# A hybrid encoder layer on one core: the second piece's token combinations made from DRAM during the first piece, the kept weights one per block, and the projection's block sums split over VectorE and GpSimd

## The chip, the cores and the metric

The kernel runs on one core of a Trainium2 chip. The metric is the device time of one execution in microseconds (us), a median over several executions. Engines are named as in the profile: PE is TensorE, PEld its weight loads, DVE or V is VectorE, ACT or S is ScalarE, POOL or G is GpSimd, SP or Q is SyncE, which only issues transfers. In the source, `V`, `S`, `G` and `Q` are the handles of these four engines, so `S.dma_start` issues a transfer from ScalarE's queue and `G.dma_start` one from GpSimd's.

## The reference, cut to what matters

One layer over 2048 prompt tokens and 32 sample tokens, in f32: a projection, attention and a gated linear attention (GLA) side by side, an output projection and a feed-forward network (FFN).

```python
z = rmsnorm(x, g_mix) @ w_in                     # D_MODEL = 1024
h = x + concat(attention(z), gla(z)) @ w_out     # 1024 x 1024
y = h + relu(rmsnorm(h, g_ffn) @ w_up)**2 @ w_down   # D_FF = 4096
```

## The kernel before, in words

Every f32 product is made as three products of rounded parts (high x high, high x low, low x high), so each operand exists as a pair of tiles whose names end in `h` and `l`. The high part is a copy by ACT, the low part a subtraction on V or POOL (`weights`, `load_tok`, `load_mix`).

The 2080 tokens are cut into three pieces p of two groups each: piece 0 has groups of 328 tokens, pieces 1 and 2 groups of 356. The FFN takes the pieces in the order `ORDER = (1, 2, 0)`, so the piece with index 2 is its second. Projection and FFN have these parts:

- **Output projection** (`op_phase`). Six groups j = 0 to 5, for (p, gi) in order; group 0's product is made earlier. For each of eight row blocks f: 24 matmuls, then V adds the residual input y (loaded by `load_y` from SP, one group ahead), ACT squares, V sums the squares into `acc`. y has three buffers, of which one is shared with memory of the stage before. `next_mix` converts the next group's attention output into `mx0` or `mx1`. After a group, `post` makes 1/rms (`oprb`, `rsqrt`), scales y (L1210) and stores what the FFN reads. It is a generator, and its parts run between the next group's steps; for the last group they run inside the FFN.
- **Token combinations.** The FFN multiplies 2 x 2 block matrices with seven products in place of eight. On the token side these are B11, B21, B22 and four differences T1 to T4. For gi = 0 `post` stores the scaled halves B11 and B21. For gi = 1 it makes all differences on V (L1220) with two copies by ACT per step, and stores T3, T1, B22, T2, T4 to the DRAM tensors `Td`.
- **Weight sums of w_down.** The weight side needs sums S1 to S4 of each of the 16 blocks b. `block_sums` makes them with four subtractions or additions on POOL and they are stored to `sd`: four early blocks and five (`MIDDLE`) in the stages before the projection (`down_sums`), the remaining seven, 9 to 15, in the projection, one begun every four steps f, all loads, sums and stores on POOL.
- **FFN** (`ffn_phase`). For each piece 16 blocks. A block has seven steps of `up` (U) and seven of `down` (D), in turn, each with 12 matmuls. After each step `prepare` makes one more pair of weights, six steps ahead: loads on SP, high part on ACT, low part on POOL, but for two of the seven down weights (`wf_dXA`, the steps 0 and 5) of the first piece's blocks 0 to 13, whose low part is made by V at L1390. The down results are added by V to the accumulators P in SBUF (L1520; L1615 copies in block 0), whose memory is shared with the tiles of the projection.
- **Kept weights.** The pairs of the last block, 15, are made once and kept in DRAM. `keep_last` makes them in four parts, in blocks 9 to 12 of the first piece, with one, two, two and two weights; the sources go through the ring `xa` of two buffers, which also carries the sources of the current down weights.
- **Start of the FFN.** In the first four down steps only one of the two PSUM buffers (`ps2[1]`) is used, since the remaining parts of `post` still use the other's banks.

The order on each engine is that of a planner that places the instructions as the code gives them with estimated times; tiles that share memory add waits.

## Time and profile before

| | us |
|---|---|
| median of three runs | 2279.6 (2277.75, 2279.6, 2291.31) |
| the profiled execution | 2273.34 |
| its span in the trace | 2271.6 |
| projection, about | 712 to 918 |
| FFN, first piece | 918 to 1425 |
| FFN, second and third piece | 1425 to 2272 |

All times of rows are microseconds from the start of the span. A row of a timeline gives the start, the busy time, the engine, the line and the tiles, how many instructions it joins, and in brackets how long the engine had been idle before it and which instruction or transfer ended that. A row of the windows gives the busy time of each engine with its instruction count, the granted clock of PE and the share and rate of the transfers.

### The profile page before, as it was taken

Reading aid. Unit: us, or ns where it says so; the run is one execution under the profiler, and the core shown is the slowest. Engines: PE = TensorE matmul, PEld = TensorE weight load, DVE = VectorE, ACT = ScalarE, POOL = GpSimd, SP = SyncE. Lnnn points to the kernel's source line nnn. Section 1 sums busy time; section 2 is a strip of 40 time slices with the busy share of each in tenths; the row PEclk is TensorE's granted clock in tenths of the full one; section 3 lists DMA queues with packets and bytes.
Section 4 is the critical chain, followed back from the end, with each engine's and each line's share of the span. In section 5 each row is a group of like instructions: output and inputs, shape, how many; then the busy total and the mean of one; then the engine's idle time right before and its main releaser. Section 6 shows DMA issues by size and latency. Waiting matters only on the chain.

```text
span 2271.6 us, 40566 instructions
## 1 busy us (share of the span) xinstructions
PE 2156.1 (95%) x14790; PEld 2023.4 (89%) x14790; DVE 1586.8 (70%) x3440; ACT 1232.3 (54%) x2728; POOL 1537.3 (68%) x1430
## 2 busy tenths in 40 slices
PE   7999999989989889799999999999999989999996
PEld 5777777778878889699999899999999989999996
DVE  8776666878887436667777776566666666766676
ACT  3545555655662212556666566665555656666662
POOL 7662224662443743678888789888887898888884
PEclk9999999989999999899999999999999999999998
DMA  7642454452235877534445547444444574444433
GB/s 257 222 173 92 153 182 153 180 179 81 101 100 193 299 252 270 215 117 140 134 138 158 172 146 294 146 142 134 140 144 132 164 267 144 140 155 146 148 112 113
DMA packets 195546, 376.34 MB, mean 166 GB/s; under 512 B 43265, under 2 KB 120370, under 8 KB 189970
## 3 DMA queue, kind: packets, MB, share of 16 engines
q1 hardware_dynamic: 172754, 293.02, 40.0%
q0 software_dynamic: 12608, 50.90, 5.9%
q10 hardware_dynamic: 9984, 29.82, 3.4%
q8 instruction: 117, 1.92, 0.4%
q14 instruction: 83, 0.68, 0.1%
HBM read 278.70 MB, written 94.98 MB: 165 GB/s over the span
## 4 chain that ended last, share of the span: by engine, by line
PE 80%; DVE 7%; DMA 5%; POOL 3%; issue 3%; ACT 2%; SPq 1%; DVEq 0%; ACTq 0%; POOLq 0%
PE dn L157 26%; PE u L157 26%; PE op L157 7%; PE zq L157 5%; PE zv L157 3%; PE zr L157 3%; PE zkv L157 2%; PE zk L157 2%; PE go L157 1%; PE O L157 1%; PE A L157 1%; DVE P L1520 1%; PE S L157 1%; SPq L60 1%; PE pT L161 1%
## 5 line engine op out<-in xcount | busy, mean ns | idle before, releaser
L1520 DVE TENSOR_TENSOR P<-P,dn 128x712 f32<-128x712 f32 (+1 forms) x642 | 559.2, 875 | 235.8 <-PE dn L157 220.2
L44 ACT ACTIVATE u<-u 128x356 f32<-128x356 f32 (+1 forms) x384 | 174.1, 453 | 58.0 <-DVE u L1520 33.9
L44 ACT ACTIVATE r<-u 128x356 f32<-128x356 f32 (+1 forms) x192 | 88.6, 462 | 137.3 <-PE u L157 137.3
L1520 DVE TENSOR_TENSOR u<-u,r 128x356 f32<-128x356 f32 (+1 forms) x144 | 75.6, 525 | 118.3 <-PE u L157 118.2
L944 POOL TENSOR_TENSOR E<-cc 128x256 f32<-128x256 f32 (+1 forms) x117 | 68.8, 624 | 92.9 <-DVE cc L796 59.7
L1415 POOL TENSOR_TENSOR stage<-stage 128x512 f32<-128x512 f32 x92 | 119.8, 1302 | 13.4 <-DMA stage<-in_w_up 8.5
L713 POOL TENSOR_TENSOR sd<-sd 128x128 f32<-128x128 f32 (+2 forms) x132 | 101.1, 782 | 29.2 <-DMA sd<-in_w_down 26.6
L1020 DVE COPY_PREDICATED AT<-masks,A 64x64 f32<-64x64 int32 (+1 forms) x330 | 82.7, 252 | 26.2 <-ACT AT L44 17.0
L1621 POOL TENSOR_TENSOR P<-P,P 128x712 f32<-128x712 f32 (+1 forms) x38 | 64.9, 1729 | 22.7 <-DVE P L1520 22.5
L44 ACT ACTIVATE P<-S,negm 128x192 f32<-128x192 f32 (+2 forms) x128 | 51.6, 417 | 46.4 <-DVE negm L578 40.9
L1283 DVE TENSOR_TENSOR y<-op,y 128x356 f32<-128x356 f32 (+1 forms) x48 | 25.0, 536 | 65.7 <-PE op L157 39.0
L44 ACT ACTIVATE E<-E 128x1024 f32<-128x1024 f32 (+2 forms) x68 | 67.3, 1013 | 1.1
L596 POOL TENSOR_TENSOR P<-P,es 128x512 f32<-128x512 f32 x15 | 15.8, 1050 | 64.2 <-ACT sq L44 22.7
L44 ACT ACTIVATE op<-y 128x356 f32<-128x356 f32 (+1 forms) x42 | 19.4, 468 | 62.2 <-DVE y L1283 62.1
L955 DVE TENSOR_TENSOR E<-E,kq 128x256 f32<-128x256 f32 (+1 forms) x117 | 52.7, 503 | 0.5 <-ACT E L44 0.3
L44 ACT ACTIVATE pS<-pT 128x256 f32<-128x256 f32 (+1 forms) x62 | 27.2, 490 | 43.7 <-PE pT L161 43.2
L1520 DVE TENSOR_TENSOR u<-u,f 128x356 f32<-128x356 f32 (+1 forms) x96 | 49.8, 519 | 0.6 <-ACT u L44 0.4
L720 POOL DMA_DIRECT2D sd<-in_w_down x56 | 36.3, 652 | 15.6 <-DMA sd<-sd 10.5
L44 ACT ACTIVATE v<-go 128x256 f32<-128x256 f32 (+1 forms) x34 | 12.8, 380 | 60.3 <-DVE Sp L1052 26.2
L577 DVE TENSOR_REDUCE mx<-S 128x2 f32<-128x384 f32 (+2 forms) x64 | 32.8, 535 | 16.9 <-PE S L157 16.6
L44 ACT ACTIVATE f<-u 128x356 f32<-128x356 f32 (+1 forms) x96 | 43.7, 455 | 0.0
L1647 POOL TENSOR_TENSOR P<-P,stage 128x712 f32<-128x712 f32 (+1 forms) x24 | 41.5, 1729 | 1.5 <-DVE P L1520 1.5
(1921 smaller groups left out, 8917.6 us busy)
## 6 DMA issues: line engine op xcount, KB each, us to landing
stage<-in_w_up SPq DMA_DIRECT2D x92, 512.0 KB, 4.0
stage<-sd SPq DMA_DIRECT2D x92, 512.0 KB, 4.6
stage<-in_w_down SPq DMA_DIRECT2D x46, 512.0 KB, 3.6
stage<-su SPq DMA_DIRECT2D x30, 512.0 KB, 3.7
sd<-in_w_down POOLq DMA_DIRECT2D x24, 512.0 KB, 6.9
sd<-sd POOLq DMA_DIRECT2D x12, 1024.0 KB, 6.5
stage<-in_w_down SPq DMA_DIRECT2D x46, 256.0 KB, 3.0
xT1a<-in_xT_prompt SPq DMA_DIRECT2D x16, 512.0 KB, 5.1
```

What stands on the lines that cost most here:

```text
L44: ins = f(*args, **kw)
L157: self._pe(self.T.matmul(out, lhsT, rhs, start=start, stop=stop, **kw), ns)
L577: V.reduce_max(mx[:, ch, us], sp, axis=AX.X)
L713: self.G.tensor_tensor(out=o, in0=x, in1=y, op=op)
L720: self.G.dma_start(raw[:, k], w[b, :, k, :, c0 : c0 + n])
L944: G.tensor_tensor(out=e4, in0=c4, in1=ref, op=ALU.subtract)
L955: V.tensor_tensor(out=e4, in0=e4, in1=halves_of(kq, L, m), op=ALU.mult)
L1020: V.copy_predicated(dst, mk.unsqueeze(1).broadcast_to([L // nh, 2, w // m, m]), src[r].rearrange("s p (n m) -> s p n m", m=m),)
L1415: tt = lambda o, x, y, op: G.tensor_tensor(out=o, in0=x, in1=y, op=op)
L1520: add = lambda out, x, y, op=ALU.add: V.tensor_tensor(out=out, in0=x, in1=y, op=op)
L1621: eng.tensor_tensor(out=e.acc[q][:, j : j + 2], in0=e.acc[q][:, j : j + 2], in1=e.acc[x][:, j : j + 2], op=ALU.add)
L1647: G.tensor_tensor(out=at, in0=at, in1=waiting.pop(g), op=ALU.add)
```

## The change

Five edits. (1) `EARLY` block sums in the GLA stage are spawned one step later with other spacing; all engines' instructions stand in the same order up to the place where the sixth block appears. (2) `MIDDLE` is 6: block 9's sums move from the projection into the GLA stage. The six blocks left in the projection are begun at other steps, four of them on VectorE and two on GpSimd, and all their loads and stores are issued by ScalarE. (3) `load_y(0, 0)` is issued after the last load of the stage before. (4) For the FFN's second piece (index 2, `LATE`), `post` only scales and stores B22 and B12, the two halves of the second group. T1 to T4 are made in blocks 10 to 13 of the first piece by `combine`: for one row block k each, four loads, four subtractions on GpSimd and four stores. With it, the start of the FFN uses both PSUM buffers. (5) `keep_last` makes one weight per block in blocks 3 to 9, through the general ring of input tiles.

```diff
-ORDER = (1, 2, 0)
-EARLY, MIDDLE = 4, 5
+ORDER, LATE = (1, 2, 0), 2
+EARLY, MIDDLE = 4, 6
...
-                if i == 3:
+                if i == 4:
...
-                        self.spawn(self.down_sums(early[j::2], one, 1, 2500), 14000 * j)
+                        self.spawn(self.down_sums(early[j::2], one, 1, 3500), 13000 * j)
...
-                self.G.tensor_tensor(out=o, in0=x, in1=y, op=op)
+                (eng or self.G).tensor_tensor(out=o, in0=x, in1=y, op=op)
...
+            if p == LATE:
+                for f in (*range(H, KB), *range(H)):
+                    scaled(y[:, f], f)
+                yield
+                S.dma_start(Td["B22"], y[:, H:])
+                S.dma_start(Td["B12"], y[:, :H])
+                return
...
-        for n, b in enumerate(range(EARLY + MIDDLE, self.NB)):
-            at = KB + 4 * n
-            steps.setdefault(at, []).append(lambda b=b: begin(b))
+        when = ((8, V), (12, V), (18, G), (24, V), (28, V), (33, G))
+        for (at, eng), b in zip(when, range(EARLY + MIDDLE, self.NB), strict=True):
+            steps.setdefault(at, []).append(lambda b=b, eng=eng: begin(b, eng))
...
-            steps.setdefault(at + 6, []).append(lambda b=b: end(b))
+            steps.setdefault(at + 5, []).append(lambda b=b: end(b))
...
-            self.load_block(x, b, 0, 512)
-            sums[b] = x, self.block_sums(x)
+            self.load_block(x, b, 0, 512, S)
+            sums[b] = x, self.block_sums(x, 1, eng)
...
-            G.dma_start(self.sd[b], sums.pop(b)[0].rearrange("p k m n -> p (k m) n"))
-
-        load_y(0, 0)
+            S.dma_start(self.sd[b], sums.pop(b)[0].rearrange("p k m n -> p (k m) n"))
+
+        with tc.issue_after(self.last_load):
+            load_y(0, 0)
...
-            pending = post(p, gi, acc, stage(f"T3{p}", N) if gi else None)
+            pending = post(p, gi, acc, stage(f"T3{p}", N) if gi and p != LATE else None)
...
+            def keep_last(i):
+
+                b, x = NF - 1, DOWN[i][0]
+                m = "S2 S3 S4 S1".split().index(x) if x[0] == "S" else int(x[1]) - 1
+                src = self.sd[b][:, m : m + 1] if x[0] == "S" else w_dn[b, :, int(x[2]) - 1 : int(x[2]), 512 * m : 512 * m + 512]
+                weights(f"d{b}{x}", load(src), True, G)
...
-                    two = ps2[1] if g == 0 and i < 4 else ps2[j // 2]
-                    ps = two.tile([P, 2, 512], F32, tag="two", name=f"dn{g}_{q}_{j}")
+                    ps = ps2[j // 2].tile([P, 2, 512], F32, tag="two", name=f"dn{g}_{q}_{j}")
...
+            def combine(k, i):
+
+                N, T = self.size(pieces[LATE][0]), self.Td[LATE]
+                names = (("B12", "B22"), ("B11", "B21"))
+                if i == 1:
+                    for pair in names:
+                        x = self.io_tile("quads")[:, : 2 * N].rearrange("p (m t) -> p m t", m=2)
+                        for j, q in enumerate(pair):
+                            quads[q] = x[:, j]
+                            Q.dma_start(x[:, j], T[q][:, k])
+                if i == 3:
+                    b12, b22, b11, b21 = (quads[q] for pair in names for q in pair)
+                    for o, x, y in ((b11, b12, b11), (b12, b22, b12), (b22, b22, b11), (b21, b21, b22)):
+                        G.tensor_tensor(out=o, in0=x, in1=y, op=ALU.subtract)
+                if i == 6:
+                    for q, t in (("B11", "T1"), ("B12", "T3"), ("B22", "T2"), ("B21", "T4")):
+                        Q.dma_start(T[t][:, k], quads.pop(q))
...
-                    if g == 0 and i in (0, 2):
+                    if g == 0 and i in (0, 2, 5):
                         next(self.pending, None)
...
-                    if g == 0 and i < 4:
-                        next(self.pending, None)
-                    if n == 0 and 9 <= b < 13 and i == 3:
-                        keep_last(b - 9)
+                    if n == 0 and 3 <= b < 10 and i == 3:
+                        keep_last(b - 3)
+                    if n == 0 and 10 <= b < 10 + H:
+                        combine(b - 10, i)
```

Three places show how the instructions move. In the rows, the name before the arrow is written and those behind it are read; the number after a name tells its copies apart.

SP's queue in the GLA stage before: y is the residual input of the projection's group 0, caf and g are inputs of the GLA tiles that follow, and y has the first place behind the normed tokens nTb.

```order
L60 DMA nTb_4l<-nTl_92 128x2048
L60 DMA y_9175<-in_xT_prompt 128x8x128
L60 DMA caf_6456<-ca_109 96x128
L60 DMA g_6081<-rgd_126 128x512
L60 DMA caf_6456<-ca_110 96x128
L60 DMA y_9175<-in_xT_prompt 128x8x128
L60 DMA y_9175<-in_xT_prompt 128x8x40
L60 DMA y_9175<-in_xT_sample 128x8x32
L60 DMA g_6615<-rgd_127 128x512
```

The same place in the changed kernel:

```order
L60 DMA nTb_4l<-nTl_92 128x2048
L60 DMA caf_6457<-ca_109 96x128
L60 DMA caf_6457<-ca_110 96x128
L60 DMA g_6082<-rgd_126 128x512
L60 DMA g_6616<-rgd_127 128x512
```

The four transfers of y(0, 0) now stand some 35 rows later, behind the last load of w_out and the GLA state's last store.

VectorE at the projection's first steps with matmuls (group 1) in the changed kernel: `op` is a product in PSUM, y_9202 the group's residual input, `sd` the block sums (L713), and `oprb` with `rsq` the 1/rms of group 0. In the kernel before, the same rows stand there without those of `sd` (such sums were on GpSimd).

```order
L1285 TENSOR_TENSOR acc_9193<-acc_9193,op_6_9105 128x328 x2
L713 TENSOR_TENSOR sd_9256<-sd_9256 128x512
L1282 TENSOR_TENSOR y_9202<-op_1_0_9224,y_9202 128x328
L713 TENSOR_TENSOR sd_9256<-sd_9256 128x512 x3
L713 TENSOR_TENSOR sd_9424<-sd_9424 128x512
L1282 TENSOR_TENSOR y_9202<-op_1_1_9259,y_9202 128x328
L713 TENSOR_TENSOR sd_9424<-sd_9424 128x512
L1203 TENSOR_SCALAR oprb<-oprb 82x4
L1285 TENSOR_TENSOR acc_9223<-acc_9223,op_1_1_9259 128x328
L713 TENSOR_TENSOR sd_9424<-sd_9424 128x512
L243 TENSOR_SCALAR oprb<-oprb 82x4
L713 TENSOR_TENSOR sd_9424<-sd_9424 128x512
```

The eight sums of two blocks now stand between the adds of y and the first steps of 1/rms on this engine.

VectorE at the start of the FFN before: the scaling (L1210) and the differences (L1220) of the last group alternate with the FFN's own work, low parts of tokens (T3l, B22l, T4l) and of squared activations (uB11l).

```order
L1518 TENSOR_TENSOR T3l<-T3l,T3h 128x712
L1210 SCALAR_TENSOR_TENSOR opa<-y_10282,packed,oprb 128x356
L1220 TENSOR_TENSOR y_10282<-opa,y_9858 128x356
L1520 TENSOR_TENSOR uB11l<-u_1_10936,uB11h 128x356
L1210 SCALAR_TENSOR_TENSOR y_10282<-y_10282,packed,oprb 128x356
L1518 TENSOR_TENSOR B22l<-B22l,B22h 128x712
L1220 TENSOR_TENSOR opa<-y_10282,opa 128x356
L1520 TENSOR_TENSOR u_2_11047<-u_0_10900,r_10735 128x356
L1518 TENSOR_TENSOR T4l<-T4l,T4h 128x712
```

The same place in the changed kernel:

```order
L1511 TENSOR_TENSOR B22l<-B22l,B22h 128x712
L1210 SCALAR_TENSOR_TENSOR y_10288<-y_10288,packed,oprb 128x356 x8
L1513 TENSOR_TENSOR uB11l<-u_1_10940,uB11h 128x356
L1513 TENSOR_TENSOR u_2_11027<-u_0_10904,r_10739 128x356
L1511 TENSOR_TENSOR T4l<-T4l,T4h 128x712
L1513 TENSOR_TENSOR u_3_10998<-u_3_10998,r_10738 128x356
```

The 16 rows of L1220 are gone, and the eight scalings stand in one piece ahead of uB11l, u_2 and T4l.

More of the change, by code (lines that the diff above doesn't have):

```diff
@@ L91, in __init__ @@
         self.Td = [
-            {x: dt([P, KB // 2, n], f"Td{p}{x}") for x in ("B11", "B21", "T2", "T1", "T3", "B22", "T4")}
+            {x: dt([P, KB // 2, n], f"Td{p}{x}") for x in ("B11", "B21", "T2", "T1", "T3", "B22", "T4", "B12")[: 8 if p == LATE else 7]}
             for p, n in enumerate(sizes)
@@ L704, in load_gla_consts, with block_sums @@
         self.gla_consts = masks, d0, wal, bal, one, ones
-    def block_sums(self, raw, parts=1):
+    def block_sums(self, raw, parts=1, eng=None):
         n = raw.shape[-1] // parts
@@ L712, in block_sums, with load_block @@
             for o, x, y, op in ((a22, a21, a22, ALU.add), (a21, a11, a21, ALU.subtract), (a11, a22, a11, ALU.subtract), (a12, a12, a11, ALU.subtract)):
-                self.G.tensor_tensor(out=o, in0=x, in1=y, op=op)
+                (eng or self.G).tensor_tensor(out=o, in0=x, in1=y, op=op)
                 yield
-    def load_block(self, raw, b, c0, n):
+    def load_block(self, raw, b, c0, n, queue=None):
         w = self.a["w_down"].rearrange("(b k p) (m n) -> b p k m n", k=2, p=P, m=2)
         for k in range(2):
-            self.G.dma_start(raw[:, k], w[b, :, k, :, c0 : c0 + n])
+            (queue or self.G).dma_start(raw[:, k], w[b, :, k, :, c0 : c0 + n])
     def down_sums(self, units, tile_, parts, step):
@@ L1229, in post, with begin @@
                 tt(y0[:, H + k], y0[:, H + k], A)
-            last = p == 2
             yield
-            eng = Q if last else S
-            eng.dma_start(Td["T3"], t3)
-            if last:
-                yield
-            eng.dma_start(Td["T1"], y[:, :H])
-            eng.dma_start(Td["B22"], y[:, H:])
-            if last:
-                yield
-            eng.dma_start(Td["T2"], y0[:, :H])
-            eng.dma_start(Td["T4"], y0[:, H:])
+            for x, src in (("T3", t3), ("T1", y[:, :H]), ("B22", y[:, H:]), ("T2", y0[:, :H]), ("T4", y0[:, H:])):
+                S.dma_start(Td[x], src)
         mix = {(0, gi): self.mix[gi] for gi in range(2)}
         steps = {}
-        for n, b in enumerate(range(EARLY + MIDDLE, self.NB)):
-            at = KB + 4 * n
-            steps.setdefault(at, []).append(lambda b=b: begin(b))
+        when = ((8, V), (12, V), (18, G), (24, V), (28, V), (33, G))
+        for (at, eng), b in zip(when, range(EARLY + MIDDLE, self.NB), strict=True):
+            steps.setdefault(at, []).append(lambda b=b, eng=eng: begin(b, eng))
             for i in (2, 3):
                 steps.setdefault(at + i, []).append(lambda b=b: more(b))
-            steps.setdefault(at + 6, []).append(lambda b=b: end(b))
+            steps.setdefault(at + 5, []).append(lambda b=b: end(b))
         sums = {}
-        def begin(b):
+        def begin(b, eng):
             x = xp.tile([P, 2048 + PADX], F32, tag="x", name=f"sd{b}")[:, :2048].rearrange("p (k m n) -> p k m n", k=2, m=2)
-            self.load_block(x, b, 0, 512)
-            sums[b] = x, self.block_sums(x)
+            self.load_block(x, b, 0, 512, S)
+            sums[b] = x, self.block_sums(x, 1, eng)
         def more(b):
@@ L1458, in up_weights @@
                 yield
-            def keep_last(part):
-                b = NF - 1
-                if part == 0:
-                    s = load(w_dn[b, :, 0:1, :512], True)
-                    weights(f"d{b}A11", s, True, G)
-                    return
-                s = load(w_dn[b, :, 1:2, :] if part == 3 else self.sd[b][:, 2 * (part == 1) : 2 * (part == 1) + 2], True)
-                names = (("S4", "S1"), ("S2", "S3"), ("A12", "A22"))[part - 1]
-                cut = (s[:, :, :512], s[:, :, 512:]) if part == 3 else (s[:, 0:1], s[:, 1:2])
-                for x, src in zip(names, cut):
-                    weights(f"d{b}{x}", src, True, G)
+            def keep_last(i):
[3 more added lines that the diff above has]
+                weights(f"d{b}{x}", load(src), True, G)
             def down_weights(n, b, out):
@@ L1633, in ffn_phase @@
             rest = [(q, gi, f) for q, gi, f0 in ((3, 1, 0), (5, 1, H), (2, 0, 0), (4, 0, H)) for f in (f0, f0 + 2)]
-            waiting = {}
+            waiting, quads = {}, {}
+            def combine(k, i):
[14 more added lines that the diff above has]
+                        Q.dma_start(T[t][:, k], quads.pop(q))
             def residual(g, i):
```

## The prediction

> **What bounds the kernel now.** I read the page first, its busy times and the chain that ended last.
>
> ```profile
> PE 2156.1 (95%) x14790; PEld 2023.4 (89%) x14790; DVE 1586.8 (70%) x3440; ACT 1232.3 (54%) x2728; POOL 1537.3 (68%) x1430
> PE 80%; DVE 7%; DMA 5%; POOL 3%; issue 3%; ACT 2%; SPq 1%; DVEq 0%; ACTq 0%; POOLq 0%
> ```
>
> TensorE (PE) is busy 95% of the span, and 80% of the chain that ended last is its matmuls. The change alters no matmul, so it can win only what PE idles and what the restarts behind idle times cost. The windows show where that is:
>
> ```profile
> 495.00:520.00 25.00, 18.20 (x182) 15.28 (x177) 15.93 (x57) 10.21 (x20) 11.71 (x18) 0.80 0.37 97
> 712.00:780.00 68.00, 58.81 (x370) 57.60 (x370) 28.45 (x70) 15.55 (x29) 48.41 (x46) 0.92 0.94 310
> 780.00:832.00 52.00, 46.17 (x293) 45.87 (x291) 23.02 (x56) 9.04 (x18) 25.40 (x23) 0.97 0.93 322
> 920.00:960.00 40.00, 31.53 (x154) 29.88 (x154) 26.06 (x58) 25.67 (x54) 30.10 (x25) 0.83 0.55 197
> 960.00:1020.00 60.00, 53.82 (x318) 53.52 (x319) 34.39 (x52) 33.08 (x68) 38.67 (x32) 0.94 0.41 144
> 1020.00:1100.00 80.00, 80.00 (x495) 80.00 (x494) 59.74 (x90) 48.29 (x102) 66.65 (x54) 1.00 0.45 143
> 1240.00:1330.00 90.00, 83.12 (x484) 82.23 (x483) 67.94 (x85) 50.04 (x107) 69.13 (x60) 0.94 0.51 167
> 1330.00:1420.00 90.00, 87.84 (x539) 87.28 (x539) 63.90 (x94) 54.91 (x113) 88.43 (x63) 1.00 0.65 234
> ```
>
> The columns are the stretch, its length, the busy time and count of PE, its loads, DVE, ACT and POOL, the granted clock, and the transfers' share and GB/s. In a quiet stretch (1020 to 1100) PE is full and there is nothing to win. The stretches the change touches leave 6.8 us idle in GLA (495 to 520), 9.2 and 5.8 in the projection, 8.5 and 6.2 at the start of the feed-forward network, and 6.9 at 1240 to 1330. The price of a restart comes from the row of the chain behind a long gap:
>
> ```profile
> 834.47 15.57 PE op L157 x80
> ```
>
> At the rate of the quiet stretch (495 matmuls in 80.00 us, 0.162 each) 80 would take 12.9 us; behind the gap they took 15.57. A restart costs up to about 2.6 us beside the gap. Twelve matmuls, a step of the network, are 1.94 us, and a block's 14 steps 27.
>
> **Early sums and y(0, 0).** The early block sums only change steps, and no engine's order changes by it up to the GLA stage: 0. In the GLA stage, y(0, 0) leaves the head of SP's queue:
>
> ```profile
> 490.44 0.56 POOL L730 DMA_DIRECT2D sd<-sd  x1 [0.30 <-POOL sd L713]
> 485.16 0.38 SPq L60 DMA_DIRECT2D nTb_4l<-nTl  x1
> 496.10 0.62 SPq L60 DMA_DIRECT2D y<-in_xT_prompt  x1
> 496.82 0.93 SPq L60 DMA_DIRECT2D caf<-ca  x1
> 497.91 3.65 DMA g<-rgd
> 501.58 0.63 ACT L44 ACTIVATE g<-g 128x512 f32<-128x512 f32 x1 [5.79 <-DMA g<-rgd]
> 503.96 0.79 PE L157 MATMUL go<-Sp,Qc 64*128 64x128 f32 x2 [6.80 <-ACT kdT L44]
> ```
>
> SP issues nothing from 485.54 to 496.10, because y's memory is that of the block sums whose store left at 490.44. Everything behind it is late: g lands at 501.56, ACT was idle 5.79 us for it, kdT stands behind g on ACT, and PE, waiting for kdT, idles 6.80. With y gone, caf and g can go some 10 us earlier, more than the gap, which should vanish. I take −8, the gap and half a restart; the ends are −9.4 (gap and full restart) and −4 (part of ACT's idle time replaced by another wait). Block 9's sums come into this stage on POOL: eight additions of 0.8 us (the next fence) in a stage where POOL has slack; I put 0, at most +2.
>
> **Block sums of the projection.** Rows of POOL's share of it and of the same operation on V:
>
> ```profile
> 483.75 6.40 POOL L713 TENSOR_TENSOR sd<-sd 128x256 f32<-128x256 f32 x8 [4.19 <-DMA sd<-in_w_down]
> 732.48 8.91 POOL L713 TENSOR_TENSOR sd<-sd 128x512 f32<-128x512 f32 x7
> 727.37 4.59 DVE L1286 TENSOR_TENSOR acc<-acc,op 128x328 f32<-128x328 f32 x3
> L1390 DVE TENSOR_TENSOR wf_d11A<-stage,wf_d11A x2: 685/3404/6123, 1251.1 to 1268.0; 128x512 fp32r<-128x512 f32 x2
> ```
>
> POOL gives up 28 additions of 1.28 us and keeps 8 of them. V gets 16; its own price for two inputs of 128x512 in SBUF is 0.69 us undisturbed, 11 us in all, in stretches where it is busy 28.45 of 68 and 23.02 of 52 us, so throughput hides them. But in group 1 eight of them stand ahead of 1/rms of group 0, for which PE waits, and their loads are now issued by ACT behind other transfers. Beside POOL's sums three such instructions of V took 1.53 us each, so the eight can also take 12. Between 0 and +5.5 (8 x 0.69) in group 1 I take +2. The twelve loads and six stores cost ACT's queue an issue each (0.4 to 0.9 us in SP's rows above), beside an ACT busy 15.55 of 68 us: 0.
>
> mx0 is written by ACT and POOL when the memory is free after group 1; POOL no longer has its DMA issues in between: −1, between −3 and +3 (ACT now issues them).
>
> The big gap of the projection follows from SP's queue and the full transfer engines:
>
> ```profile
> 805.34 8.62 SPq L60 DMA_DIRECT2D y<-in_xT_prompt  x4
> 814.06 1.73 SPq L60 DMA_DIRECT2D m<-mixT  x1
> 815.88 1.99 SPq L60 DMA_DIRECT2D stage<-in_w_up  x2
> 817.97 11.00 SPq L60 DMA_DIRECT2D y<-in_xT_prompt  x4
> 833.89 2.70 DVE L1283 TENSOR_TENSOR y<-op,y 128x356 f32<-128x356 f32 x6 [15.40 <-DMA y<-in_xT_prompt]
> 834.47 0.67 PE L157 MATMUL op<-mx1h,wo10h 128*128 128x356 f32 x1 [8.30 <-DVE y L1283]
> 814.28 0.56 POOL L1266 DMA_DIRECT2D sd<-sd  x1 [0.30 <-POOL sd L713]
> ```
>
> V lacked y(1, 1) until 833.6, and PE ran out of PSUM for 8.30 us. The transfers are at 0.93 of their time; issuing eight loads of y took SP 19.6 us. The last store of block sums, 1 MB, left at 814.28. In the changed kernel one block (1 MB in, 1 MB out, at 322 GB/s 6.5 us of transfer time) is gone, the last block begins at f = 33 in place of 32 but without POOL's order ahead of it, and one w_up load fewer stands ahead of y(1, 1). Against that the 1.3 MB of y(0, 0) (328 tokens of 4 KB) move into the start of this stretch, 4 us at the same rate. Removing the gap and a restart would give −10.9; −2 is the net of 6.5 and 4. I take −9, nearer to the first, since y(2, 0) moves ahead of two mixT loads and so leaves SP free earlier.
>
> **Second piece at the FFN's start.** Three gaps:
>
> ```profile
> 947.44 0.43 PE L157 MATMUL dn<-uB11h,wf_d0A 128*128 128x356 f32 x1 [2.84 <-ACT P L44]
> 954.14 0.43 PE L157 MATMUL dn<-uB22h,wf_d0S 128*128 128x356 f32 x1 [0.99 <-DVE P L1615]
> 956.48 0.93 SPq L60 DMA_DIRECT2D Td2T<-T  x1
> 964.37 0.90 DVE L1615 COPY P<-dn 128x712 f32<-128x712 f32 x1 [3.83 <-DMA Td2T<-T]
> 965.32 0.66 PE L157 MATMUL dn<-uT1h,wf_d0S 128*128 128x356 f32 x1 [7.03 <-DVE P L1615]
> L1210 DVE SCALAR_TENSOR_TENSOR y<-y,packed,oprb x7: 578/579/581, 899.8 to 954.5; 128x356 f32<-128x356 f32 x7
> ```
>
> The 7.03 come from V's copy into P, which waits 7.77 us (956.48 to 964.25) for the store of T3, whose memory it is. In the changed kernel there is no T3 tile for this piece, so this wait has no source: −7.0 and a restart, −2.6. The 2.84 and 0.99 are waits for the single PSUM buffer in use; with both in use the next product has a place: −3.8. Against that, V does eight scalings of 0.58 us, 4.6 us, in one piece ahead of uB11l, u_2 and T4l, where today they are spread, so each of the three can be up to 4.6 us later; half a microsecond of it on PE's path is my guess, since V is busy 26.06 of 40 us there: +0.5. The stores of B22 and B12 leave right behind the scalings. Sum −13; ends −9 (only the T3 wait) and −17 (the 14.7 us of idle time between 920 and 1020 and a restart).
>
> The four combinations come back in blocks 10 to 13 of the first piece: four subtractions on POOL of 0.95 us (z in the next fence has the same shape), 3.8 per block of 27 us, two tiles of the input ring, and eight transfers on SP, of which the four stores wait for POOL, ahead of w_down and w_up loads. POOL and SP work six steps, 11.6 us, ahead. From 1330 to 1420 POOL is busy 88.43 of 90 us and PE 87.84: even a full POOL costs 2 us. I put 0 to +3, and take 0.
>
> **Kept weights.**
>
> ```profile
> L1290 POOL TENSOR_TENSOR z<-y x12: 873/954/1560, 746.5 to 920.4; 128x356 f32<-128x356 f32 x8, 128x328 f32<-128x328 f32 x4
> 1248.92 6.99 DMA stage<-sd
> 1256.72 1.29 POOL L1390 TENSOR_TENSOR wf_d11S<-stage,wf_d11S 128x512 fp32r<-128x512 f32 x1 [2.46 <-ACT wf_d11S L44]
> 1275.41 0.43 PE L157 MATMUL dn<-uT3h,wf_d11S 128*128 128x356 f32 x1 [3.33 <-DVE P L1520]
> 1307.80 0.66 PE L157 MATMUL dn<-uT3h,wf_d12S 128*128 128x356 f32 x1 [3.33 <-DVE P L1520]
> ```
>
> Twice PE idles 3.33 us. The first time V's low part wf_d11A (at 1268.0, the row above) took 6.12 us instead of 0.69, while POOL worked off back to back what had waited since the late load of `sd` through the two-buffer ring. With one kept weight per block and another ring this pile does not form: two gaps and two restarts, −11.9 at most. But POOL now has 1.29 + 0.57 us more in each of blocks 3 to 9, where it is at 0.83, so some of V's slow splits will turn up there. I take −7; ends −11.9 and +6 (one new gap and restart, nothing gained).
>
> A rule to weigh: the Trainium skill, page "SBUF — State Buffer", section "Who interferes with whom", says that a VectorE instruction with two SBUF inputs contends with a GpSimd instruction that reads SBUF, and that the other blocks until the first finishes. By it V would wait for one POOL instruction, about 1.3 us, so that a split could take 2 us and open no gap; the 6.12 us are more than four POOL instructions long, so here the trace does not bear out that the loser waits for one only. By the rule alone this term would be 0.
>
> **Sum:** −8 + 2 − 1 − 9 − 13 − 7 = −36. Against the profiled execution, 2273.3 − 36 = 2237; that one is 6.3 below the median of the runs shown, 2279.6, so I forecast 2279.6 − 36 = 2244.
>
> **Rivals.** (B) *The projection stays limited by its transfers.* y(0, 0) moves from an idle queue into a stretch with a transfer share of 0.94, ACT issues the sums' loads late, and V waits for them ahead of 1/rms. For it: the shares. Against: a net of 0.7 MB less. The −9 goes, group 1 costs 5 instead of 2, mx0 +1 instead of −1: −36 + 9 + 3 + 2 = −22, 2258.
> (C) *VectorE starves beside GpSimd*, the other side. Blocks 3 to 13 each have two low parts on V, 22 of them, while POOL goes from 0.83 to above 0.9. If in 11 of them V loses as at 1268, each costs 3.33 + 2.6 = 5.9 us: +65, the 7 of the kept weights are not won: 2244 + 72 = 2316. It breaks even at five such events (29 + 7 = 36). For it: two of four blocks did so. Against: with POOL at 0.98 (1330 to 1420) PE lost only 2 us.
> (D) *The gap at the FFN's start only moves*: the copy into P finds another store (B12) or the scalings ahead of T4l hold PE. The −9.6 of the T3 wait goes and 2 come: −24, 2256.
> (E) *All goes at its better end*: −9.4, 0, −3, −10.9, −17, −11.9 would be −52; with some of it lost again perhaps −46, 2234.
>
> **How the numbers follow.** Chances: my forecast 0.48 (2236 to 2252), B 0.18, D 0.16, E 0.10, C 0.08, of which 0.04 to its end above. A measurement can tell about 1%, 23 us, from no change: faster is below 2256.8, slower above 2302.4. Faster: 0.48 + 0.10 + half of B and D, 0.17, together 0.75. Slower: half of C, 0.04. Within 1%: 0.21. The range runs from 2230, E with 4 us to spare, to 2268, which holds B and D with 10 us of what they may add; it leaves out C and the ends of the others, some 0.15.
>
> **What would show it.** Right: no gap near 497 and g on ACT right behind its transfer; V's adds of y in group 3 not waiting for y(1, 1); the first four copies into P without a transfer ahead; no gap of 3 us in blocks 11 and 12, and V's splits in blocks 3 to 13 near 0.7 us. Wrong: PE idle in blocks 3 to 13 with V's split at several us behind a full POOL (C); 1/rms of group 0 late behind the sums (B); T4l late, or P behind a store (D).

## The result and the profile after

| | before | after |
|---|---|---|
| median of 16 runs each | 2278.93 us | 2265.03 us |
| the profiled execution, span | 2273.34, 2271.6 | 2254.98, 2252.9 |
| ratio of the runs, 95% interval | | 0.9922 [0.9899, 0.9945] |

The change wins 14 us by the medians, 0.6%, and 0.8% by the ratio: clear of noise, within 1%. One execution in sixteen of the changed kernel (2968.94 us), one of e1 and one of e7 were slow ones; the ratios leave them out, and so do the medians given below. The forecast was 36 us, 2244. The measured 2265 lies in the stated range, 2230 to 2268, but 3 us from its end, and a win of less than 1% had been given a chance of 0.21.

The two profiled executions lie 18.7 us apart, and how that comes about can be read off PE, since it works through the same matmuls in the same order. Of the kernel before there is one trace, 5.6 us faster than its median, so every difference to before is one to this execution. Up to 484.78, where the change alters no engine's order, the traces of the other twelve kernels stand between −2.0 and +3.5 us against it. The table gives how much earlier (negative) the changed kernel starts the same matmul, worked out from the first rows of the same names in PE's timelines.

| place | before starts at | after, against before |
|---|---|---|
| GLA, query projection of the fourth normed tile | 484.78 | 0.0 |
| same, zk<-nTb_3h | 508.64 | −8.0 |
| GLA, key projection of the fifth normed tile | 538.33 | −5.7 |
| projection, group 0 | 668.43 | −5.7 |
| projection, second half of group 2 | 785.28 | +5.5 |
| projection, group 4 | 844.66 | −2.9 |
| projection, second half of group 5 | 902.37 | −3.3 |
| first piece, block 0, last product | 982.98 | −15.8 |
| block 9, last product | 1228.66 | −9.4 |
| block 12, last product | 1322.37 | −15.9 |
| block 14, last product | 1376.85 | −13.8 |
| third piece, last block | 2254.35 | −17.3 |

So the start of the feed-forward network wins what was forecast, GLA about two thirds of it, and in two places the changed kernel gives time back: 11 us in the projection's first groups, and some of it again and again in the first piece. The profile's first lines and the gaps in front of PE's matmuls, from the page and PE's timeline of the changed kernel:

```profile
PE 2147.9 (95%) x14790; PEld 2013.7 (89%) x14790; DVE 1615.1 (72%) x3440; ACT 1228.8 (55%) x2720; POOL 1526.4 (68%) x1416
PE 74%; DVE 12%; DMA 5%; POOL 3%; issue 3%; ACT 2%; SPq 1%; ACTq 0%; DVEq 0%; POOLq 0%
...
723.07 0.46 PE L157 MATMUL op<-m1h,wo00h 128*128 128x328 f32 x1 [4.50 <-ACT op L44]
740.11 1.80 PE L157 MATMUL oprb<-packed,rsq_y_y 82*128 82x82 f32 x8 [3.82 <-DVE rsq_y_y L248]
833.86 0.43 PE L157 MATMUL op<-mx1h,wo10h 128*128 128x356 f32 x1 [2.16 <-DVE y L1282]
939.11 0.66 PE L157 MATMUL u<-T4l,wf_u0A 128*128 128x356 f32 x1 [5.22 <-DVE T4l L1511]
1132.84 0.64 PE L157 MATMUL dn<-uB21h,wf_d6A 128*128 128x356 f32 x1 [1.92 <-DVE P L1513]
1237.31 0.43 PE L157 MATMUL dn<-uT3h,wf_d10S 128*128 128x356 f32 x1 [2.37 <-DVE P L1513]
```

The gaps of 6.80 (GLA), 7.03, 2.84 and 0.99 (start of the network) and the two of 3.33 (blocks 11 and 12) are gone but for 0.91 of the last, and that of 8.30 has become 2.16. Five others of more than 1.9 us are new. Four of them name VectorE, and VectorE's share of the chain went from 7% to 12%. Its timeline and GpSimd's side by side at 5.22 and at 2.37 show why:

```profile
933.05 6.00 DVE L1511 TENSOR_TENSOR T4l<-T4l,T4h 128x712 fp32r<-128x712 f32 x1
932.92 1.30 POOL L1389 TENSOR_TENSOR wf_d0S<-stage,wf_d0S 128x512 fp32r<-128x512 f32 x1
934.16 1.70 POOL L1511 TENSOR_TENSOR T4l<-T4l,T4h 128x712 fp32r<-128x712 f32 x1
935.80 1.27 POOL L1389 TENSOR_TENSOR wf_u1S<-stage,wf_u1S 128x512 fp32r<-128x512 f32 x1
937.02 1.26 POOL L1414 TENSOR_TENSOR stage<-stage 128x512 f32<-128x512 f32 x1
940.59 1.28 POOL L1389 TENSOR_TENSOR wf_d0S<-stage,wf_d0S 128x512 fp32r<-128x512 f32 x1 [2.31 <-ACT wf_d0S L44]
...
1222.08 0.89 DVE L1513 TENSOR_TENSOR P<-P,dn 128x712 f32<-128x712 f32 x1
1230.23 5.78 DVE L1389 TENSOR_TENSOR wf_d10A<-stage,wf_d10A 128x512 fp32r<-128x512 f32 x1
1229.88 0.95 POOL L1641 TENSOR_TENSOR quads<-quads 128x356 f32<-128x356 f32 x1
1230.79 1.28 POOL L1389 TENSOR_TENSOR wf_d10S<-stage,wf_d10S 128x512 fp32r<-128x512 f32 x1
1232.04 2.52 POOL L1389 TENSOR_TENSOR wf_u11S<-stage,wf_u11S 128x512 fp32r<-128x512 f32 x2
1234.53 0.93 POOL L1641 TENSOR_TENSOR quads<-quads 128x356 f32<-128x356 f32 x1
1238.78 1.28 POOL L1389 TENSOR_TENSOR wf_d10A<-stage,wf_d10A 128x512 fp32r<-128x512 f32 x1 [3.32 <-ACT wf_d10A L44]
```

Both instructions of VectorE read two inputs from SBUF. T4l is started 0.13 us behind a GpSimd instruction and ends at 939.05, 0.77 us after GpSimd's run of four ends at 938.28. The low part wf_d10A ends at 1236.01, 0.55 us after the run ends at 1235.46. Undisturbed they take 0.9 and 0.69 us. In both places VectorE's turn came only when GpSimd paused, after four and five of its instructions. VectorE's adds into P, with one input in PSUM, run at their usual 0.9 us beside the same run (0.89 at 1222.08).

It does not always take a pause. In block 11 of the same trace VectorE got in behind GpSimd's second instruction:

```profile
1261.21 1.28 POOL L1389 TENSOR_TENSOR wf_u12S<-stage,wf_u12S 128x512 fp32r<-128x512 f32 x1
1261.72 2.25 DVE L1389 TENSOR_TENSOR wf_d11A<-stage,wf_d11A 128x512 fp32r<-128x512 f32 x1
1262.46 0.95 POOL L1641 TENSOR_TENSOR quads<-quads 128x356 f32<-128x356 f32 x1
1263.38 1.74 POOL L1389 TENSOR_TENSOR wf_u12S<-stage,wf_u12S 128x512 fp32r<-128x512 f32 x1
```

No pause shows between the last two rows; the last took 1.74 us instead of 1.29, with the end of VectorE's instruction inside it. In the thirteen traces in which VectorE makes low parts of the first piece's down weights, 125 of them took more than 1.2 us. While they waited, GpSimd 84 times paused for 0.05 us or more between two instructions, and VectorE got in each time. At 220 ends of a GpSimd instruction without such a pause it got in 41 times and was passed over 179 times. So a pause lets VectorE in, and without one it can wait for a single instruction or for the whole run; what decides that is not shown.

### The profile page after: what moved, and what is told of

Same layout as the page of the kernel before. It is cut to its first block, busy times and chain, and to the rows that moved or that the text cites. A ratio compares the mean times of both kernels' runs of the same rounds, so it can differ in the third digit from the quotient of the medians.

```text
span 2252.9 us, 40626 instructions
## 1 busy us (share of the span) xinstructions
PE 2147.9 (95%) x14790; PEld 2013.7 (89%) x14790; DVE 1615.1 (72%) x3440; ACT 1228.8 (55%) x2720; POOL 1526.4 (68%) x1416
## 4 chain that ended last, share of the span: by engine, by line
PE 74%; DVE 12%; DMA 5%; POOL 3%; issue 3%; ACT 2%; SPq 1%; ACTq 0%; DVEq 0%; POOLq 0%
PE dn L157 25%; PE u L157 25%; PE op L157 5%; PE zq L157 5%; PE zr L157 3%; PE zv L157 2%; PE zkv L157 2%; DVE AT L1020 1%; PE zk L157 1%; PE O L157 1%; DVE E L955 1%; PE go L157 1%; SPq L60 1%; PE A L157 1%; DMA y<-in_xT_prompt 1%
## 5 line engine op out<-in xcount | busy, mean ns | idle before, releaser
L713 POOL TENSOR_TENSOR sd<-sd 128x128 f32<-128x128 f32 (+2 forms) x120 | 85.0, 724 | 46.5 <-DMA sd<-in_w_down 43.9
L955 DVE TENSOR_TENSOR E<-E,kq 128x256 f32<-128x256 f32 (+1 forms) x117 | 58.8, 555 | 0.6 <-ACT E L44 0.5
L844 POOL TENSOR_TENSOR g<-g,ggla 128x512 f32<-128x512 f32 (+1 forms) x17 | 22.2, 1316 | 28.6 <-ACT g L44 28.6
```

The costliest lines, as they stand in the source:

```text
L713: (eng or self.G).tensor_tensor(out=o, in0=x, in1=y, op=op)
L955: V.tensor_tensor(out=e4, in0=e4, in1=halves_of(kq, L, m), op=ALU.mult)
```

## The experiments

All kernels are edits of the changed one. Beside each median stands the ratio to before with its interval. As executions of one kernel scatter by 10 us and more, the tests go by PE's progress in the stretch that the edit touches.

**Whose fault is the projection's loss?** Three edits: the queue of the block transfers, the engine of the first two blocks' sums, and both.

```diff
# e1_pool_queue
-            self.load_block(x, b, 0, 512, S)
+            self.load_block(x, b, 0, 512, G)
...
-            S.dma_start(self.sd[b], sums.pop(b)[0].rearrange("p k m n -> p (k m) n"))
+            G.dma_start(self.sd[b], sums.pop(b)[0].rearrange("p k m n -> p (k m) n"))
# e2_first_two_pool
-        when = ((8, V), (12, V), (18, G), (24, V), (28, V), (33, G))
+        when = ((8, G), (12, G), (18, G), (24, V), (28, V), (33, G))
```

The kernel e7_three_pool has the engines of e2, and the queue of e1 for the blocks below 13.

> The changed kernel with the loads and stores of the projection's six blocks issued by GpSimd again, as before; the sums stay where the change puts them. In the changed kernel's trace ScalarE's sequencer needs 6.67 us (714.42 to 721.19) for three of these loads, its squares behind them are late, and PE idles 4.50 us at 718.57 because PSUM is not freed. Theory A (ScalarE's issues hold its own work): that gap goes and with it a restart, 4 to 6 us less than the changed kernel, and ScalarE is not idle 7 us in front of op. Theory B (it is the full transfer engines, 0.95 busy there, that hold every queue): the loads of y and m stay late, the gap only changes place, and the time stays within 2 us.

> The changed kernel with the sums of blocks 10 and 11 on GpSimd, all transfers still issued by ScalarE. Theory A (the eight sums on VectorE stand ahead of 1/rms of group 0 and delay it): the gap of 3.82 us at 736.29 in front of oprb goes and with it about 4 us of slow matmuls, 6 to 8 us less than the changed kernel. Theory B (1/rms is late only because its inputs are late behind ScalarE's issues): the gap stays within 1 us, and the time within 2 us.

> The changed kernel with the sums of blocks 10 to 12 on GpSimd and their transfers issued by GpSimd, blocks 13 to 15 as the change has them. Theory A (both ScalarE's issues and VectorE's sums cost in group 1): between the last step of group 0 and the first matmul of group 2, where the changed kernel loses 8 to 12 us against before, the loss is below 3 us, and the gap in front of group 3 stays near 2 us; 6 to 9 us less than the changed kernel. Theory B (the moved load of y is what delays group 1): 6 us or more of the loss stay.

Medians 2259.54 (0.9915 [0.988, 0.995]), 2257.87 (0.9903 [0.9864, 0.9941]) and 2252.88 (0.9895 [0.9862, 0.9927]). From group 0 to the second half of group 2 (668.4 to 785.3) the changed kernel lost 11.2 us against before, and in seven other executions with this part unaltered (the runs e3, e4, e5, e6, e8, f2 and f3) 7.0 to 10.3, 9.1 on average over the eight. e1 lost 5.2, e2 7.0, e7 2.0.

ScalarE's issues are one cause: e1 rid PE of the gap of 4.50 (theory A), which stays in e2 (4.94). VectorE's sums are the other: e2 rid PE of the gap of 3.82 in front of the product with rsq_y_y (theory A), although one of 1.54 opened ahead of it, where acc is late. The 7.0 of e2 by itself proves nothing, since one of the unaltered executions lost as little; but e7 loses 3.3 us less than e1. The changed kernel's rows of ScalarE and VectorE:

```profile
714.42 6.67 ACTq L44 DMA_DIRECT2D sd<-in_w_down  x3
721.19 0.44 ACT L44 ACTIVATE op<-op 128x328 f32<-128x328 f32 x1 [7.49 <-DMA y<-in_xT_prompt]
721.67 0.50 DVE L1282 TENSOR_TENSOR y<-op,y 128x328 f32<-128x328 f32 x1 [8.75 <-ACT op L44]
...
728.92 5.79 DVE L713 TENSOR_TENSOR sd<-sd 128x512 f32<-128x512 f32 x4
727.80 6.37 POOL L713 TENSOR_TENSOR sd<-sd 128x512 f32<-128x512 f32 x4 [23.93 <-DMA sd<-in_w_down]
```

ScalarE's sequencer needed 6.67 us for three issues while the transfers were at 0.91 of their time, and its own squares stood behind them. The bracket names a transfer of y, but the row above shows that ScalarE was not waiting for it: it was issuing. In e7 that gap is 0.53 us instead of 4.50. The sums themselves take 1.45 us each on VectorE beside GpSimd's instead of 0.69: here the two engines take turns, one instruction each. In e1 a new gap of 3.85 opened, since VectorE's last sum of squares stood behind an add that waited 3.41 us for y: theory B has a part in it.

e7 met the first half of its expectation and not the second: 5.38 us are left in front of op<-mx1h in group 3 (5.20 in e2), where y(1, 1) again has two loads of w_up ahead of it on SP's queue instead of one, and its four issues take 10.33 us instead of the changed kernel's 7.09. In group 1 a gap of 2.56 in front of the product with rsq_y_y is left too, behind an add that waits 8.60 us for y.

**How many blocks does the projection stand, and what does block 9 cost in GLA?**

```diff
# f1_seven, on top of e7
-EARLY, MIDDLE = 4, 6
+EARLY, MIDDLE = 4, 5
...
+        when = ((8, G), (12, G), (16, G), (20, G), (24, V), (28, V), (33, G))
```

> The kernel of the run e7_three_pool with block 9's sums back in the projection (seven blocks there, the first four on GpSimd), so that GpSimd has no sixth block in the GLA stage. Theory A (block 9's sums on GpSimd make VectorE's E<-E,kq slow, since it reads two inputs in SBUF, and this gives back most of what the earlier caf and g win): from the query projection of the fourth normed tile to the key projection of the fifth (484.8 to 538.3 before), where nine profiled executions so far changed by -5.6 to +2.1 us against before, -1 on average, this one is 7 to 10 us shorter than before. Theory B (block 9 costs 2 us at most): 3 us shorter or less, as on average so far, and the delay has another cause.

Median 2255.38 (0.9906 [0.9869, 0.9944]). The stretch of GLA came out 9.0 us shorter than before: theory A. With block 9 in GLA, the changed kernel and the ten experiments that leave this part alone stand at −0.8 on average, and the changed kernel's own −5.6 was the best of the eleven. The rows of the changed kernel, then of f1:

```profile
512.06 5.12 POOL L713 TENSOR_TENSOR sd<-sd 128x256 f32<-128x256 f32 x6
513.34 4.54 DVE L955 TENSOR_TENSOR E<-E,kq 128x256 f32<-128x256 f32 x6
```

```profile
509.53 2.17 DVE L955 TENSOR_TENSOR E<-E,kq 128x256 f32<-128x256 f32 x6
828.62 0.67 PE L157 MATMUL op<-mx1h,wo10h 128*128 128x356 f32 x1 [9.04 <-DVE y L1282]
```

VectorE's six multiplications, with two inputs in SBUF, take 4.54 us beside block 9's sums and 2.17 without. Later matmuls wait for the chain that they start. The price of taking block 9 back is in the second row: with seven blocks in the projection the gap of group 3 is at 9.04 us, against 5.38 in e7, on which f1 is built, and 2.16 in the changed kernel. So the block less is worth some 3.7 us of this gap, and some 3.2 come with the sums of blocks 10 and 11 on VectorE, with which only one load of w_up stands ahead of y(1, 1).

**Kept weights and combinations.**

```diff
# e3_old_keep
-                    if n == 0 and 3 <= b < 10 and i == 3:
-                        keep_last(b - 3)
+                    if n == 0 and 9 <= b < 13 and i == 3:
+                        keep_last(b - 9)
# e4_no_split
-                eng.tensor_tensor(out=l3, in0=src, in1=f32(h3), op=ALU.subtract)
+                if eng is V:
+                    S.activation(l3, src, AF.Copy)
+                else:
+                    eng.tensor_tensor(out=l3, in0=src, in1=f32(h3), op=ALU.subtract)
# e5_no_combine
-                    for o, x, y in ((b11, b12, b11), (b12, b22, b12), (b22, b22, b11), (b21, b21, b22)):
-                        G.tensor_tensor(out=o, in0=x, in1=y, op=ALU.subtract)
```

In e3 keep_last itself is also that of before.

> The changed kernel with the kept weights made as before, in four parts in blocks 9 to 12 through the ring of two buffers. Theory A (spreading them costs in blocks 4 to 10 what it gains in 11 and 12): the losses of 1.2, 5.3 and 4.2 us that the changed kernel has in blocks 4, 6 and 10 shrink to at most 4 in all, those of blocks 11 and 12 come back with 10 us or more, and the time is within 5 us of the changed kernel. Theory B (as forecast, spreading wins 7): 7 us slower than the changed kernel. Theory C (the combinations in blocks 10 to 13 are what costs, and with the old parts on top GpSimd is overrun): 15 us slower or more.

> The changed kernel with the low part of the two down weights per block that VectorE makes replaced by a copy of the source on ScalarE; the subtraction is left out, for blocks 0 to 13 of the first piece. Theory A (VectorE's instruction with two inputs in SBUF gets its turn only when GpSimd pauses, so PE waits for VectorE's adds behind it): the gaps at 1073, 1131, 1235, 1294 and 1322 go, and the first piece is 12 to 16 us shorter than in the changed kernel. Theory B (GpSimd itself is late with weights, and VectorE's wait only shows it): gaps of the same sum remain, now in front of weights, and the first piece is less than 4 us shorter.

> The changed kernel with the four subtractions per block of the second piece's combinations left out (blocks 10 to 13 of the first piece); their loads and stores stay. Theory A (GpSimd's load starves VectorE's low parts): the losses of blocks 10 and 13 (4.2 and 2.0 us in the changed kernel) go, those of blocks 4 to 6 (1 to 6 us, from the kept weights) stay; about 6 us less than the changed kernel. Theory B (the extra transfers and the input ring are what is late): the losses of blocks 10 and 13 stay within 1 us.

Medians 2270.38 (0.9952 [0.9925, 0.998]), 2253.24 (0.9889 [0.9851, 0.9926]) and 2256.03 (0.9887 [0.9847, 0.9927]). Against before, in us by the same matmuls of the first piece (from the end of block 0 to the end of block 9, and from there to the end of block 14):

| | blocks 1 to 9 | blocks 10 to 14 |
|---|---|---|
| changed kernel | +6.4 | −4.4 |
| e3, kept weights as before | 0.0 | +14.4 |
| e4, no subtraction on VectorE | +1.8 | −11.8 |
| e5, no combinations on GpSimd | +1.1 | −11.8 |

−11.8 is all that blocks 11 and 12 had lost before. Without the combinations' sixteen subtractions blocks 10 to 14 lose nothing, and without VectorE's 28 low parts nothing either, though GpSimd then still has all its work: it is not GpSimd's lateness, but VectorE's wait. So theory A holds for e4 in these blocks, which are 12.0 us shorter than in the changed kernel; the start of the network won only 5.0 us in it, where T3l's half on VectorE took 6.50 us and 1/rms of the last group behind it held PE 5.37. For e5 theory A holds in blocks 10 and 13, but the losses of blocks 4 to 6 did not stay (1.2 us instead of 6.5). With the old parts on top of the combinations (e3) a low part took 10.95 us; blocks 10 and 13 lost 9 us each, and the kernel is 12 us slower than the changed one in this piece and 5 by the medians, nearest to theory B; its trace is that of the slowest of its ten executions. Blocks 1 to 9 scatter between executions of the changed arrangement, from +1.1 to +7.7. The windows of the changed kernel and of e5, blocks 10 to 13:

```profile
1205.00:1335.00 130.00, 124.93 (x757) 124.05 (x756) 102.39 (x131) 73.88 (x157) 115.53 (x98) 0.99 0.55 179
```

```profile
1205.00:1335.00 130.00, 130.00 (x803) 130.00 (x802) 95.43 (x142) 79.29 (x169) 109.29 (x89) 1.00 0.56 184
```

GpSimd at 0.89 of the time leaves PE 5 us idle, at 0.84 none.

**When does VectorE get its turn?**

```diff
# e8_pause
+                    if n == 0 and not made and eng is G:
+                        G.memset(src[x][:, :, :1], 0.0)
# f3_step6
-                    eng = V if n == 0 and i in (0, 5) and b < NF - 2 else G
+                    eng = V if n == 0 and i in (0, 6) and b < NF - 2 else G
```

> The changed kernel with a fill of one column per part behind each low part of a down weight that GpSimd makes in the first piece; the fill writes a source tile that is no longer needed and reads nothing. Theory A (VectorE's instruction with two inputs in SBUF gets its turn when GpSimd has an instruction that does not read SBUF): VectorE's low parts of blocks 4 to 13 take at most 2.5 us each, and the first piece is 6 to 12 us shorter than in the changed kernel. Theory B (VectorE waits until GpSimd has nothing left to do): some of them still take 4 to 6 us, and the first piece is as long or longer, by what the fills add.

> The changed kernel with the second of VectorE's two low parts per block moved from the down weight of step 5 to that of step 6; GpSimd makes the one of step 5. Theory A (what costs is where VectorE's instruction falls in GpSimd's run without a pause; step 6 falls in the pause of 2 to 3 us that GpSimd has behind step 5): VectorE's low parts take less than 2 us, and blocks 4 to 13 of the first piece are 5 us or more shorter than in the changed kernel. Theory B (any place in a block is as bad): the same sum of losses within 3 us, at other steps.

Medians 2262.49 (0.9913 [0.988, 0.9946]) and 2259.52 (0.9896 [0.9858, 0.9935]). In e8 the rows of VectorE and GpSimd around the second low part of block 10:

```profile
1240.71 5.47 DVE L1389 TENSOR_TENSOR wf_d10A<-stage,wf_d10A 128x512 fp32r<-128x512 f32 x1 [1.34 <-POOL stage L1484]
1244.38 1.25 POOL L1389 TENSOR_TENSOR wf_u12A<-stage,wf_u12A 128x512 fp32r<-128x512 f32 x1
1245.58 0.09 POOL L1484 MEMSET stage<- 128x1 f32 x1
1246.29 0.95 POOL L1643 TENSOR_TENSOR quads<-quads 128x356 f32<-128x356 f32 x1 [0.62 <-DMA quads<-Td2B]
...
1213.41 3.56 DVE L1389 TENSOR_TENSOR wf_d10A<-stage,wf_d10A 128x512 fp32r<-128x512 f32 x1
1215.07 0.10 POOL L1484 MEMSET stage<- 128x1 f32 x1
1216.49 1.61 POOL L1414 TENSOR_TENSOR stage<-s,stage 128x512 f32<-128x512 f32 x1
```

The 5.47 us end in GpSimd's pause of 0.62 us. The fill at 1215.07 let nobody in: VectorE's instruction ended at 1216.97, behind the next GpSimd instruction, where GpSimd stood still for 0.08 us and its following one took 1.61 us instead of 1.29. VectorE was passed over in the same way at the fills of 1102.89 and 1131.25. At 1074.92 and 1159.83 VectorE did get in behind the fill, without a pause of GpSimd:

```profile
1158.86 1.58 DVE L1389 TENSOR_TENSOR wf_d8A<-stage,wf_d8A 128x512 fp32r<-128x512 f32 x1
...
1159.83 0.10 POOL L1484 MEMSET stage<- 128x1 f32 x1
1159.88 1.72 POOL L1389 TENSOR_TENSOR wf_u9A<-stage,wf_u9A 128x512 fp32r<-128x512 f32 x1
```

So a fill of 0.1 us does not reliably open the way, and whether it helped in these two places is not shown, as VectorE gets in at other ends of instructions too. A pause opens it, even a short one. Theory A is refuted: four low parts of blocks 4 to 13 still took 2.95 to 5.47 us. All blocks from 1 to 14 together come to +0.2 in e8 against +2.0, and −2.4 to +3.7 in the seven experiments that leave these blocks alone, so the fills neither won nor cost anything that shows. f3 has the same sum of losses in blocks 4 to 13 within 3 us (0 against +2), with one low part of 9.34 us in block 11: theory B, step 6 is no safer than step 5.

**The gap in front of T4l.**

```diff
# e6_late_scaling
-                    if g == 0 and i in (0, 2, 5):
+                    if g == 0 and i in (0, 4, 6):
# f2_t4_pool
-                load_tok(envs[0], t, (V, G), Q if t in ("B11", "B21") else S)
+                load_tok(envs[0], t, (G, G) if t == "T4" else (V, G), Q if t in ("B11", "B21") else S)
```

> The changed kernel with the eight scalings of the last group two steps later in the feed-forward network's first block, so that five of them stand behind T4l on VectorE and uB11l and u_2 ahead of all. Theory A (the scalings ahead of T4l hold PE): the gap of 5.22 us at 933.89 in front of u<-T4l shrinks by 2 us or more and a part of the restart goes, 3 to 6 us less than the changed kernel. Theory B (T4l is late by its high part on ScalarE or by GpSimd's half): the gap stays within 1 us.

> The changed kernel with both halves of T4l of the first piece made by GpSimd instead of one by VectorE. Theory A (VectorE's half takes 6.00 us instead of 0.90 because GpSimd runs back to back): the gap in front of u<-T4l (5.2 us) shrinks to 4 us or less, now with GpSimd as the one waited for, and VectorE's next instructions come 5 us earlier; 1 to 4 us less than the changed kernel. Theory B (T4l is late by its transfer or its high part): the gap stays within 0.5 us.

Medians 2257.68 (0.9892 [0.9848, 0.9936]) and 2258.67 (0.9906 [0.9874, 0.9939]). In e6, T4l has only three scalings ahead, and the gap stays at 5.36. VectorE's half takes 5.85 us. In f2, where VectorE has no half, the gap is 2.00, and from block 0's product with T2 to that of block 1 PE wins 15.1 us against before instead of 10.3. The expectation for e6 named the wrong alternative too: neither the scalings nor the high part hold T4l.

**All three together.**

```diff
# g_best, on top of e7 and f2
+            if b == EARLY + MIDDLE - 1:
+                with self.tc.issue_after(self.e_last[8]):
+                    self.load_block(raw, b, c0, n)
```

Here `e_last` holds GpSimd's last E instruction of each half tile, so block 9's sums fall behind VectorE's multiplications.

> The kernel of the run e7_three_pool (blocks 10 to 12 of the projection on GpSimd), with both halves of T4l on GpSimd and with block 9's load in the GLA stage issued only behind the E tiles of the fourth normed tile, so that its eight sums fall behind VectorE's E<-E,kq. Theory A (VectorE's instructions with two inputs in SBUF starve beside GpSimd's runs, and each of the three places can be taken out by itself): from the fourth normed tile's query projection to the fifth's key projection 6 to 9 us shorter than before, the gap in front of u<-T4l at 2 us; together about 2243 us, 1.6% less than before, 9 to 12 us less than the run e7_three_pool. Theory B (the gains in the GLA stage and in front of T4l are lost again where the next engine is late): within 5 us of the run e7_three_pool.

Median 2251.7 (0.9888 [0.9851, 0.9926]), the lowest of all, though its interval overlaps that of every other edit. The GLA stretch came out 9.0 us shorter, as expected, and the six multiplications take 2.16 us again. But the network's start won no more than in e7 (15.0 and 14.5 us against before), and the total missed theory A's by 9 us and fell to theory B's side:

```profile
508.47 2.16 DVE L961 TENSOR_TENSOR E<-E,kq 128x256 f32<-128x256 f32 x6
...
917.56 6.20 DVE L1517 TENSOR_TENSOR B22l<-B22l,B22h 128x712 fp32r<-128x712 f32 x1
923.69 0.15 DVE L247 SCALAR_TENSOR_TENSOR oprb<-oprb,rsq_y_y 89x4 f32<-89x4 f32 x1
```

Now B22l, half on VectorE too, falls into a run of GpSimd, takes 6.20 us, and holds the 1/rms of the last group behind it: 4.74 us of PE. It does so in e7 already, where T4l, with its half still on VectorE, is not late:

```profile
926.80 6.22 DVE L1511 TENSOR_TENSOR B22l<-B22l,B22h 128x712 fp32r<-128x712 f32 x1
...
940.32 0.89 DVE L1511 TENSOR_TENSOR T4l<-T4l,T4h 128x712 fp32r<-128x712 f32 x1
```

With e7's edits in the projection the wait had moved from T4l to B22l, so f2's edit had nothing left to win. A gain that was measured on top of one arrangement need not be there on top of another.

## Why the prediction came out as it did, by its own steps

| term | forecast | measured | from |
|---|---|---|---|
| early sums | 0 | 0 | 484.78 |
| y(0, 0) and block 9 in GLA | −8 | −5.6 here, −0.8 on average of eleven | 484.8 to 538.3 |
| group 1 and mx0 | +2 − 1 | +11.2 here, +9.1 on average of eight | 668.4 to 785.3 |
| y(1, 1) in group 3 | −9 | −8.4 | 785.3 to 844.7 |
| start of the network | −13 | −12.5 | 902.4 to 983.0 |
| kept weights | −7 | −5.4 (−11.8 and +6.4) | blocks 11, 12; 1 to 9 |
| combinations | 0 | +7.4 | blocks 10 to 14, against e5 |

By the averages where there are several the sum is −0.8 + 9.1 − 8.4 − 12.5 − 5.4 + 7.4, about −11; the changed kernel's median lies 8.3 us below this execution of before. By the profiled execution's own values it is −13.3, and the rest of its −18.7 came where nothing was changed, above all 5.8 us between the second piece's start and the third piece's end. Three terms (block 9, group 1, the combinations) make 23 of the 25 us by which the forecast of −36 missed the −11. That 2265 still lies in the range is owed to the range's width, drawn for rivals B and D, and not to the sum.

- **y(0, 0): right; block 9: wrong.** The gap of 6.80 went, as argued from SP's row. "I put 0, at most +2" for block 9 failed. Its eight additions were priced by GpSimd's slack, though the row of VectorE's acc at 1.53 us, quoted two steps later, had shown what GpSimd's run does to such an instruction. f1 and g_best, where they are away from VectorE's multiplications, win 9.0, within the forecast's ends.
- **Group 1: both bounds missed.** The sums were put between 0 and 5.5 us, with the 12 us mentioned and not used. "The twelve loads and six stores cost ACT's queue an issue each" went by SP's undisturbed issues, 0.4 to 0.9 us, although the rows quoted for group 3 had SP at 8.62 and 11.00 us for four issues under the same load. That was the nearer row: three issues took 6.67. (GpSimd gives up 20 of its 28 additions there, not 28; no term rests on this.)
- **Group 3: right** in size (−8.4), and both things that it named have a part: f1 against e7 puts some 3.7 us of the gap on the block less, and the one w_up load fewer ahead of y(1, 1), which e2 and e7 lose again, goes with some 3.2.
- **Start of the network: right in size, by two errors.** The three gaps went, and with them other losses of the stretch; T4l then cost 5.22 and a restart of up to 2.6, so that what went must have been some 20 us. The step had put half a microsecond there and blamed the scalings ahead; e6 and f2 show VectorE's own half of T4l.
- **Kept weights: right** in the mechanism and near in size: −11.8 won, a part lost in blocks 4 to 9, as the step says. That part scatters, from +1.1 to +7.7, so the −5.4 is one draw of it.
- **Combinations: wrong.** The cover named was a full GpSimd from 1330 to 1420 where "PE lost only 2 us". In that stretch VectorE makes one low part, at its very start (2.28 us at 1333.39), and none after it, since blocks 14 and 15 have none: the evidence came from a stretch almost without the mechanism.
- **Rivals.** C was the mechanism that decided, with a chance of 0.08 and the wrong argument against it. It came as smaller events, of 1 to 5 us, and in GLA, the projection and at T4l too, not in blocks 3 to 13 alone. B's two mechanisms in group 1 came true at once, its gap in group 3 did not. D's late T4l came true beside the T3 wait's end, but it was not the scalings that held it.

## What to carry to other kernels

Price an instruction added to GpSimd by what VectorE has to run beside it, not by GpSimd's free time: in these kernels a VectorE instruction with two SBUF inputs that fell into a GpSimd run waited for one of its instructions at best and for the whole run at worst, and what stood behind it waited too. Ask of a stretch that is quoted as cover whether the mechanism in question occurs in it at all. Before an engine is given transfers to issue, read how long issues take in that stretch, not elsewhere, and what of the engine's own stands behind them.

## What the runs showed of the hardware

VectorE's subtraction of two SBUF tiles took 0.68 us alone and up to 10.95 us (e3) and 9.34 (f3) beside GpSimd's unbroken runs for 128x512, and 0.9 alone and up to 6.50 (T3l in e4) for 128x712. Where it waited for the run's end, it ended 0.5 to 0.8 us behind the last instruction. GpSimd's instructions in such a run start 1.25 us apart while each lasts 1.29. The Trainium skill, page "SBUF — State Buffer", section "Who interferes with whom", has the contention, and says that the one that is second blocks until the first finishes. The runs agree on who contends. On how long they agree where VectorE got in behind one instruction, as beside the block sums of the projection (1.45 us each), and not at the 179 ends of an instruction where GpSimd's next one went first.

The granted clock of stretches with gaps was lower (0.90 from 700 to 785, against 1.00 at 970 to 1062), and a part of the losses in the tables is slow matmuls behind a gap, not idle time: PE's gaps grew by 9.4 us where the projection lost 11.2, and by 3.8 where blocks 1 to 9 lost 6.4.
